# The first of two kinds of VectorE additions in a joint weight set no longer pinned to the order of the program

## The chip, the cores and the metric

The kernel runs on one core of a Trainium2 chip. The metric is the device time of one execution in microseconds (us); lower is better. The engines are TensorE (PE in the profile; its weight loads are PEld), VectorE (DVE), ScalarE (ACT), GpSimd (POOL) and SyncE (SP); the last two mostly issue DMAs here.

## The reference

One layer of a decoder trunk on 256 tokens with a width of 2048, in float32. Cut to what matters:

```python
h = rmsnorm(x, pre_norm_g)
proj = h @ w_in                       # (256, 2048) @ (2048, 18448)
a_q, a_k, a_v, a_g, a_lr, b_q, b_k, b_v, b_g, m_a, m_b = split(proj)
y_a = (rmsnorm(gla_chunked(a_q, a_k, a_v, gk)) * silu(a_g)) @ w_branch_a
y_b = (rmsnorm(diff_attention(b_q, b_k, b_v, lam)) * silu(b_g)) @ w_branch_b
merged = sigmoid(m_a) * y_a + sigmoid(m_b) * y_b
x = x + rmsnorm(merged @ w_out, post_norm_g)
```

The change is in the projection `h @ w_in`, which takes over half of the kernel's time.

## The kernel before, in words

Every matrix product is made of three products of rounded numbers: a weight tile is split into `hi` (a copy on ScalarE into the rounded type float32r, line 354) and `lo` (the tile minus `hi`, on VectorE, line 355), and TensorE multiplies the activations with both (line 551, a helper called for nearly all matmuls). Such a tile has 128 partitions and mostly 1024 columns. The tiles for `hi` and `lo` rotate through three buffers each, and the conversion runs three steps ahead of TensorE (`AHEAD`).

Nine stretches of the projection, the *sets* 0 to 8 (lines 220 to 261 and `block_products`), use a scheme that needs seven block products instead of eight: the 2048 x 1024 weights of a set are four blocks, and some products take sums of blocks. The seven products run in the order 1, 3, 5, 6, 2, 7, 4; each has four steps, written here as (product, t, h) with t and h of 0 or 1: t is a half of the block's rows and selects a tile, h a half of that tile's columns. Between a set's steps come steps of other column groups (`phase_steps`), whose raw tiles need no sums: in the profile they write banks named `bg`, the set's own `mm`.

The sums of weight blocks are made in place. For each t, a tile `a` is loaded with the first block and a tile `b` with the fourth (`link`), `c` with the third.

- After step (1, t, h) the second block is added to `a` by an accumulating DMA that POOL issues (line 249): (5, t, h) then reads `a`.
- After products 3 and 5 have read them, VectorE adds `b`, the fourth block, to `a` (line 257). Product 6 reads `a` then. This is called when the step in the table of `follow_set` has been written out: the additions for t = 0, halves h = 0 and 1, at (5, 1, 0) and (5, 1, 1); those for t = 1 at (6, 0, 0) and (6, 0, 1). Behind each, an accumulating DMA on POOL adds the second block to `b`, for product 7.
- At (7, t, h) VectorE adds `c`, the third block, to `a` (line 257 too), for product 4.

A scheduler orders each engine's instructions by its own model, so the order in which the program is written sets it only in part. `tc.keep_in_program_order(i)` pins an instruction behind the one that was written before it on its engine. TensorE's matmuls of this phase are all pinned so, as are POOL's DMAs, and in the kernel before all additions of line 257. The other names of the rows below are `q` and `k` (L793 to L796), results of the steps in between, `p` (L871, a copy of the bank of product 1 or 5 by ScalarE, and L874, a sum of such copies on VectorE), `gr` (L878 and L887, finished halves of a set), and L868 (ScalarE copies the bank of product 1 when that product is done, in sets 1 to 8). Line 291 is another addition of weight tiles, in the last part of the kernel.

Of the kernel before, what the change touches and what calls it, by code (L numbers as in the profile page):

```python
# [11 lines left out]
ALU = mybir.AluOpType  # L12
# [130 lines left out]
def hybrid_kernel(ctx: ExitStack, tc, xt, xn, preg, postg, w, w2, gkb, glag, lamv, diffg, ident_d, causal_d, lmask_d, out):  # L143
    nc = tc.nc
    pe, act, dve, pool, sp = nc.tensor, nc.scalar, nc.vector, nc.gpsimd, nc.sync
# [66 lines left out]
    raws = {}  # L212
    chain = {}
# [5 lines left out]
    def block(s, i, t):  # L219
        return weights(f"set{s}", 2 * i + t)[0]  # L220
# [24 lines left out]
    def follow_set(s, prod, t, h):  # L245
        c = slice(1024 * h, 1024 * h + 1024)

        def accumulate(name, i):
            tc.keep_in_program_order(pool.dma_start(chain[s, name, i][:, c], block(s, 1, i)[:, c], accum_op=ALU.add))  # L249

        if prod == 1:
            accumulate("a", t)
        i = {(5, 1): 0, (6, 0): 1, (7, 0): 0, (7, 1): 1}.get((prod, t))
        if i is not None:
            a = chain[s, "a", i][:, c]
            second = prod != 7
            tc.keep_in_program_order(dve.tensor_tensor(out=a, in0=a, in1=chain[s, "b", i][:, c] if second else raws[s, i, h], op=ALU.add))  # L257
            if second:
                accumulate("b", i)

    def part_link(s, name, make=u2):
        first, second = {"b": (3, None), "f": (3, 1), "e": (1, 0)}[name]
        for h in range(2):
            c = slice(1024 * h, 1024 * h + 1024)
            t = chain[s, name, h] = make([P, 1024], f"part_{name}")
            tc.keep_in_program_order(sp.dma_start(t, weights(s, first)[0][:, c]))
            if second is not None:
                tc.keep_in_program_order(pool.dma_start(t, weights(s, second)[0][:, c], accum_op=ALU.add))
# [53 lines left out]
    def emit_half():  # L322
# [33 lines left out]
        if joined:  # L356
            follow_set(*e[1:])
# [1215 lines left out]
    for c in range(2):  # L1573
# [12 lines left out]
        else:  # L1586
            end = ps("bg")
            c = slice(TURNED[0] % 1024, TURNED[0] % 1024 + 512)
# [68 lines left out]
```

## Time and profile before

| | |
|---|---|
| Time, median of 3 runs | 1090.64 us (1090.23 to 1091.9) |
| The profiled execution | 1089.85 us, its span 1088.0 us |
| TensorE busy | 1077.3 us (99%) |
| VectorE busy | 947.8 us (87%) |
| ScalarE busy | 742.4 us (68%) |
| POOL busy | 168.2 us (15%) |
| Granted TensorE clock | 0.999 of full speed |
| DMA | 293.44 MB, mean 270 GB/s |

A row of the timeline reads: start, duration, engine, line, operation, what it writes and reads, shapes, how many such instructions follow each other, and in brackets the idle time of the engine before it and what ended that. VectorE's and ScalarE's instructions overlap a little, so an instruction of 1.22 us can start 1.14 us behind the one in front. A row of the chain reads: start, duration, what. TensorE counts as busy while a matmul is in its pipeline, so its 99% don't mean that it lost only 1%; lost time is seen in the starts of its matmuls. The sets run from about 85 to 600 us.

### The profile page before, as it was taken

How to read it: one execution, taken by the hardware profiler on the slowest of the kernel's cores; microseconds unless marked ns; L12 is line 12 of the kernel's file. 1: busy time of each engine (PE TensorE's matmuls, PEld its weight loads, DVE VectorE, ACT ScalarE, POOL GpSimd, SP SyncE). 2: the span in 40 equal slices, each digit the busy share in tenths (PEclk: the TensorE clock that was granted, in tenths of full speed). 3: DMA queues.
4: the chain of work that ended last, by engine and by line, in shares of the span. 5: the costliest groups of instructions: out<-in, count | busy, mean ns of one | idle time of the engine just before them, and what ended most of it. 6: DMA issues, size and time to landing. Idle time of an engine off the chain costs nothing.

```text
span 1088.0 us, 15371 instructions
## 1 busy us (share of the span) xinstructions
PE 1077.3 (99%) x5404; PEld 918.0 (84%) x5404; DVE 947.8 (87%) x1282; ACT 742.4 (68%) x1068; POOL 168.2 (15%) x249
## 2 busy tenths in 40 slices
PE   9999999999999999999999999999999999999997
PEld 8998887878887888888888888888888888888886
DVE  7788989889998989898989899987778878879886
ACT  7987767777676767767776655566777776566662
POOL 0202121111212111212212210031011011100000
PEclk9999999999999999999999999999999999999999
DMA  8899799999897989898989776599897798988752
GB/s 347 271 340 285 226 288 283 256 269 300 230 344 173 358 184 374 197 335 218 316 240 273 273 258 202 194 321 315 277 299 257 272 297 269 325 300 260 273 190 99
DMA packets 67213, 293.44 MB, mean 270 GB/s; under 512 B 8704, under 2 KB 11776, under 8 KB 49984
## 3 DMA queue, kind: packets, MB, share of 16 engines
q1 hardware_dynamic: 38656, 174.29, 45.3%
q0 software_dynamic: 27904, 117.45, 40.2%
q8 instruction: 42, 0.69, 0.2%
q10 hardware_dynamic: 576, 0.73, 0.2%
q14 instruction: 35, 0.29, 0.1%
HBM read 265.17 MB, written 27.26 MB: 269 GB/s over the span
## 4 chain that ended last, share of the span: by engine, by line
PE 89%; DVE 5%; issue 2%; DMA 2%; ACT 1%; POOL 0%; POOLq 0%; SPq 0%; DVEq 0%; ACTq 0%
PE mm L551 60%; PE bg L551 18%; DVE lo L355 3%; PE mm L539 2%; PE bg L539 2%; DMA a<-in_w_dram 1%; DVE a L257 1%; PE mm L524 1%; PE bg L980 1%; PE bg L524 1%; PE bg L1147 0%; PE bg L1121 0%; DMA raw<-in_w_dram 0%; PE bg L1122 0%; PE bg L1159 0%
## 5 line engine op out<-in xcount | busy, mean ns | idle before, releaser
L354 ACT ACTIVATE hi<-raw 128x1024 fp32r<-128x1024 f32 (+3 forms) x229 | 234.6, 1028 | 148.9 <-PE mm L551 73.4
L355 DVE TENSOR_TENSOR lo<-raw,hi 128x1024 fp32r<-128x1024 f32 (+3 forms) x231 | 271.3, 1180 | 34.9 <-ACT hi L354 31.9
L354 ACT ACTIVATE hi<-a 128x1024 fp32r<-128x1024 f32 x144 | 152.5, 1060 | 63.1 <-PE mm L551 25.4
L355 DVE TENSOR_TENSOR lo<-a,hi 128x1024 fp32r<-128x1024 f32 x144 | 172.7, 1222 | 19.5 <-ACT hi L354 17.0
L551 PE MATMUL mm<-hi,xs 128*128 128x512 f32 (+1 forms) x688 | 174.8, 383 | 0.0
L551 PEld LDWEIGHTS mm<-hi,xs 128*128 128x128 f32 x688 | 128.5, 188 | 21.4
L551 PE MATMUL bg<-xs,hi 128*128 128x512 f32 x448 | 115.7, 390 | 0.0
L355 DVE TENSOR_TENSOR lo<-b,hi 128x1024 fp32r<-128x1024 f32 x72 | 88.0, 1223 | 18.0 <-ACT hi L354 15.9
L551 PE MATMUL mm<-lo,xs 128*128 128x512 f32 (+1 forms) x344 | 98.7, 383 | 0.1
L551 PEld LDWEIGHTS bg<-xs,hi 128*128 128x128 f32 x448 | 84.3, 188 | 16.6
L354 ACT ACTIVATE hi<-b 128x1024 fp32r<-128x1024 f32 x72 | 76.1, 1060 | 25.5 <-PE mm L551 13.5
L551 PE MATMUL mm<-xs,hi 128*128 128x512 f32 x320 | 84.9, 397 | 0.0
L551 PEld LDWEIGHTS mm<-lo,xs 128*128 128x128 f32 x344 | 64.2, 188 | 12.2 <-DVE lo L355 1.3
L551 PEld LDWEIGHTS bg<-xs,lo 128*128 128x128 f32 x448 | 60.3, 190 | 10.5 <-DVE lo L355 6.8
L551 PE MATMUL bg<-xs,lo 128*128 128x256 f32 x448 | 63.5, 285 | 2.6 <-DVE lo L355 2.4
L551 PEld LDWEIGHTS mm<-xs,hi 128*128 128x128 f32 x320 | 57.7, 189 | 9.6
L249 POOL DMA_DIRECT2D b<-in_w_dram x36 | 31.0, 861 | 169.1 <-ACT hi L354 70.1
L354 ACT ACTIVATE hi<-c 128x1024 fp32r<-128x1024 f32 x36 | 38.2, 1062 | 21.0 <-PE bg L551 9.7
L551 PE MATMUL mm<-hi,oah 128*128 128x512 f32 x128 | 50.9, 397 | 0.0
L551 PE MATMUL mm<-hi,oal 128*128 128x512 f32 x128 | 50.1, 391 | 0.0
L551 PEld LDWEIGHTS mm<-xs,lo 128*128 128x128 f32 x320 | 43.7, 190 | 3.2
L551 PE MATMUL mm<-xs,lo 128*128 128x256 f32 x320 | 44.6, 283 | 0.0
(410 smaller groups left out, 2218.6 us busy)
## 6 DMA issues: line engine op xcount, KB each, us to landing
raw<-in_w_dram SPq DMA_DIRECT2D x98, 1024.0 KB, 7.0
c<-in_w_dram SPq DMA_DIRECT2D x36, 512.0 KB, 8.4
a<-in_w_dram POOLq DMA_DIRECT2D x36, 512.0 KB, 9.8
b<-in_w_dram POOLq DMA_DIRECT2D x36, 512.0 KB, 8.4
a<-in_w_dram POOLq DMA_DIRECT2D x16, 1024.0 KB, 10.6
b<-in_w_dram POOLq DMA_DIRECT2D x16, 1024.0 KB, 7.9
raw<-in_w_dram SPq DMA_DIRECT2D x14, 832.0 KB, 7.1
gr<-gr POOLq DMA_DIRECT2D x9, 512.0 KB, 10.1
```

The lines of the kernel that those rows point to most:

```text
L249: tc.keep_in_program_order(pool.dma_start(chain[s, name, i][:, c], block(s, 1, i)[:, c], accum_op=ALU.add))
L257: tc.keep_in_program_order(dve.tensor_tensor(out=a, in0=a, in1=chain[s, "b", i][:, c] if second else raws[s, i, h], op=ALU.add))
L354: act.activation(hi_t[:, a:b], r[:, a:b], AF.Copy)
L355: dve.tensor_tensor(out=lo_t[:, a:b], in0=r[:, a:b], in1=f32(hi_t[:, a:b]), op=ALU.subtract)
L524: i = pe.matmul(out, lhs, rhs, start=first and n == 0, stop=last and n == len(pairs) - 1, **kw)
L539: i = pe.matmul(banks[g][b][:, :n], a[part][:, P * b : P * b + P], w[:, n * g : n * g + n], start=first, stop=last)
L551: i = pe.matmul(*args, **kw)
L980: pe.matmul(o, xk[:, P * c : P * c + P], xq.rearrange("p (b c t) -> p b c t", b=2, c=4)[:, :, c, :], start=i == 0, stop=i == 1)
```

## The change

Of the additions of line 257, only those of `c` (at product 7) are still pinned. Those of `b`, with which the sums for product 6 are made, are left to the scheduler.

```diff
@@ follow_set
             second = prod != 7
-            tc.keep_in_program_order(dve.tensor_tensor(out=a, in0=a, in1=chain[s, "b", i][:, c] if second else raws[s, i, h], op=ALU.add))
+            add = dve.tensor_tensor(out=a, in0=a, in1=chain[s, "b", i][:, c] if second else raws[s, i, h], op=ALU.add)
             if second:
                 accumulate("b", i)
+            else:
+                tc.keep_in_program_order(add)
```

The order of TensorE, POOL and SP stays. Lines behind 257 have their numbers raised by 2 in the changed kernel (355 becomes 357). VectorE in set 2 before, from the lo's of (5, 0, 0) and (5, 0, 1) on; `a_1712` is the tile of t = 0, `a_1826` that of t = 1, `raw` a tile of the steps in between:

```order
L355 TENSOR_TENSOR lo_2056<-a_1712,hi_2055 128x1024
L355 TENSOR_TENSOR lo_2066<-a_1712,hi_2065 128x1024
L355 TENSOR_TENSOR lo_2078<-a_1826,hi_2077 128x1024
L257 TENSOR_TENSOR a_1712<-a_1712,b_1871 128x1024
L794 TENSOR_TENSOR q_2012<-bg_2013,q_2012 128x2x128
L355 TENSOR_TENSOR lo_2107<-a_1826,hi_2106 128x1024
L257 TENSOR_TENSOR a_1712<-a_1712,b_1871 128x1024
L355 TENSOR_TENSOR lo_2119<-raw_2102,hi_2118 128x1024
L355 TENSOR_TENSOR lo_2131<-a_1712,hi_2130 128x1024
```

And in the changed kernel:

```order
L357 TENSOR_TENSOR lo_2056<-a_1712,hi_2055 128x1024
L257 TENSOR_TENSOR a_1712<-a_1712,b_1871 128x1024
L357 TENSOR_TENSOR lo_2066<-a_1712,hi_2065 128x1024
L257 TENSOR_TENSOR a_1712<-a_1712,b_1871 128x1024
L357 TENSOR_TENSOR lo_2078<-a_1826,hi_2077 128x1024
L796 TENSOR_TENSOR q_2012<-bg_2013,q_2012 128x2x128
L357 TENSOR_TENSOR lo_2107<-a_1826,hi_2106 128x1024
L357 TENSOR_TENSOR lo_2119<-raw_2102,hi_2118 128x1024
L357 TENSOR_TENSOR lo_2131<-a_1712,hi_2130 128x1024
```

Each addition now stands right behind the lo that reads its half of the tile last. Sets 4 and 6 are ordered in the same way. In sets 1, 3, 5 and 7 the two additions go up by one row each, in set 0 the first by two rows and the second by one, and in set 8 only the first, by two. In sets 3 and 5 the first addition of t = 1 also goes up by one row.

VectorE in product 7 of set 7, where `gr` is the addition of line 887 and `raw` the tile of a step in between, before:

```order
L257 TENSOR_TENSOR a_4312<-a_4312,c_4634 128x1024
L887 TENSOR_TENSOR gr_4742<-mm_4451,p_301_4648 128x512
L355 TENSOR_TENSOR lo_4848<-raw_4776,hi_4847 128x1024
L355 TENSOR_TENSOR lo_4870<-a_4189,hi_4869 128x1024
L355 TENSOR_TENSOR lo_4880<-a_4189,hi_4879 128x1024
```

And in the changed kernel:

```order
L257 TENSOR_TENSOR a_4312<-a_4312,c_4634 128x1024
L357 TENSOR_TENSOR lo_4848<-raw_4776,hi_4847 128x1024
L889 TENSOR_TENSOR gr_4742<-mm_4451,p_301_4648 128x512
L357 TENSOR_TENSOR lo_4870<-a_4189,hi_4869 128x1024
L357 TENSOR_TENSOR lo_4880<-a_4189,hi_4879 128x1024
```

The lo of the raw tile passes the addition that finishes a half of the set.

ScalarE in set 2, from the hi of a raw tile to that of the next, before:

```order
L354 ACTIVATE hi_2118<-raw_2102 128x1024
L354 ACTIVATE hi_2130<-a_1712 128x1024
L871 ACTIVATE p_157_2156<-mm_2101 128x512
L354 ACTIVATE hi_2144<-a_1712 128x1024
L354 ACTIVATE hi_2161<-raw_2102 128x1024
```

And in the changed kernel, as also in sets 4 and 6:

```order
L356 ACTIVATE hi_2118<-raw_2102 128x1024
L356 ACTIVATE hi_2130<-a_1712 128x1024
L356 ACTIVATE hi_2144<-a_1712 128x1024
L873 ACTIVATE p_157_2156<-mm_2101 128x512
L356 ACTIVATE hi_2161<-raw_2102 128x1024
```

The copy of product 5's bank goes behind the hi of (6, 0, 1).

## The prediction

> **What bounds the kernel now.** I read the page first, then the times of one ScalarE row that comes once in every set, then the timeline of VectorE, ScalarE and TensorE at one place. The page, with the chain that ended last:
>
> ```profile
> span 1088.0 us, 15371 instructions
> ...
> PE 89%; DVE 5%; issue 2%; DMA 2%; ACT 1%; POOL 0%; POOLq 0%; SPq 0%; DVEq 0%; ACTq 0%
> ```
>
> TensorE carries 89% of the chain, so a shorter VectorE or DMA is worth nothing except where TensorE stands and waits for it. What can be won is therefore the time that TensorE loses in the sets, and this is found by a clock inside the kernel. Line L868 (a bank copied when product 1 of a set is done) runs once in each of the sets 1 to 8, right behind TensorE. The columns are start, duration, and the instruction:
>
> ```profile
> 148.95 0.58 ACT L868 ACTIVATE mm<-mm 128x512 f32<-128x512 f32 x1
> 207.91 0.58 ACT L868 ACTIVATE mm<-mm 128x512 f32<-128x512 f32 x1
> 266.80 0.58 ACT L868 ACTIVATE mm<-mm 128x512 f32<-128x512 f32 x1
> 324.43 0.58 ACT L868 ACTIVATE mm<-mm 128x512 f32<-128x512 f32 x1
> 383.65 0.58 ACT L868 ACTIVATE mm<-mm 128x512 f32<-128x512 f32 x1
> 441.29 0.58 ACT L868 ACTIVATE mm<-mm 128x512 f32<-128x512 f32 x1
> 500.89 0.58 ACT L868 ACTIVATE mm<-mm 128x512 f32<-128x512 f32 x1
> 559.12 0.58 ACT L868 ACTIVATE mm<-mm 128x512 f32<-128x512 f32 x1
> ```
>
> The differences are 58.96, 58.89, 57.63, 59.22, 57.64, 59.60 and 58.23 us for the sets 1 to 7. The matmuls of these sets are equal in number and shape. Sets 3 and 5 agree at 57.63, which I take as the period without a stall. The others lose 1.33, 1.26, 1.59, 1.97 and 0.60, together 6.75 us, and no later set gives any of it back.
>
> Where set 2 loses it is seen on VectorE around products 5 and 6. Call (5,0,1) the step with product 5, t = 0, h = 1:
>
> ```profile
> 214.91 2.58 DVE L355 TENSOR_TENSOR lo<-a,hi 128x1024 fp32r<-128x1024 f32 x2
> 219.49 1.23 DVE L355 TENSOR_TENSOR lo<-a,hi 128x1024 fp32r<-128x1024 f32 x1 [2.00 <-ACT hi L354]
> 220.63 1.22 DVE L257 TENSOR_TENSOR a<-a,b 128x1024 f32<-128x1024 f32 x1
> ...
> 222.10 1.22 DVE L355 TENSOR_TENSOR lo<-a,hi 128x1024 fp32r<-128x1024 f32 x1
> 223.24 1.22 DVE L257 TENSOR_TENSOR a<-a,b 128x1024 f32<-128x1024 f32 x1
> 224.37 1.22 DVE L355 TENSOR_TENSOR lo<-raw,hi 128x1024 fp32r<-128x1024 f32 x1
> ...
> 228.91 1.22 DVE L257 TENSOR_TENSOR a<-a,b 128x1024 f32<-128x1024 f32 x1
> 230.04 0.69 DVE L874 TENSOR_TENSOR p<-mm,p 128x512 f32<-128x512 f32 x1
> 230.65 1.22 DVE L355 TENSOR_TENSOR lo<-raw,hi 128x1024 fp32r<-128x1024 f32 x1
> ```
>
> The first row is the lo of (5,0,0) and (5,0,1); then VectorE stands idle for 2.00 us until ScalarE brings the hi of (5,1,0). From there to 231.9 it runs without a gap, with one instruction of 128x1024 every 1.14 us. Four additions (L257) are in this stretch. TensorE over the same time, and from the chain the time of a block of 16 that waits for nothing:
>
> ```profile
> 220.49 0.62 PE L551 MATMUL mm<-lo,r1h 128*128 128x512 f32 x2
> ...
> 229.62 1.78 PE L551 MATMUL bg<-xs,hi 128*128 128x512 f32 x7
> 231.92 1.22 PE L551 MATMUL bg<-xs,lo 128*128 128x256 f32 x8 [0.52 <-DVE lo L355]
> ...
> 233.21 0.40 PE L551 MATMUL mm<-hi,s2h 128*128 128x512 f32 x1
> ...
> 188.17 2.77 PE bg L551 x16
> ```
>
> TensorE takes the lo of (5,0,1) at 220.49, 3.0 us after VectorE had it (214.91 + 2.58 = 217.49). The block of 16 from 229.62 to 233.21 took 3.59 instead of 2.77 us, since its lo came at 231.87, the end of the last VectorE row above. So VectorE is 3 us ahead, idles, and 14 us later is late by 0.8 us.
>
> **The change part by part.** No instruction is added or removed except two that only wait; TensorE's, POOL's and SP's orders stay. VectorE's moves, and three pairs on ScalarE.
>
> *Sets 2, 4 and 6.* The two additions of half h = 0 and h = 1 go in front of the lo of (5,1,0). Requeued for set 2 with the spacings of the rows: lo (5,0,0) ends at 216.14; addition 216.17 to 217.39; lo (5,0,1) 217.31 to 218.53, still 2.0 us ahead of TensorE's 220.49; second addition 218.56 to 219.78, so the hole of 2.00 is filled; lo (5,1,0) at 219.70 instead of 219.49; after it the first addition is missing from the row, so lo (5,1,1) comes at 221.17 instead of 222.10, and the raw lo, without the second, at 222.31 instead of 224.37. From there on everything is 2.06 us earlier as long as ScalarE is. ScalarE:
>
> ```profile
> 222.09 1.06 ACT L354 ACTIVATE hi<-a 128x1024 fp32r<-128x1024 f32 x1 [0.35 <-PE mm L551]
> 224.15 0.60 ACT L871 ACTIVATE p<-mm 128x512 f32<-128x512 f32 x1 [0.99 <-PE mm L551]
> ...
> 225.97 1.06 ACT L354 ACTIVATE hi<-raw 128x1024 fp32r<-128x1024 f32 x1 [0.28 <-PE bg L551]
> ```
>
> The hi of the last raw lo is there at 227.03, so that lo can start at 228.6 and end at 229.8. TensorE asks for it after eight matmuls of hi, about 231.0 by the rows above and some 0.4 earlier when its own small stalls before (1.26 - 0.82) are gone. It is ahead by 0.8 us, and the stall goes. The swap on ScalarE (p behind the hi of (6,0,1)) delays p by about 1.0 us, to 225.8; its reader on VectorE (L874, 230.04, then about 228) is later still, so it costs nothing. Worth: 1.26 for set 2 and 1.59 for set 4. Set 6 has the same order as set 4; I take 1.59 of its 1.97 and leave the rest, which I don't ascribe to this place.
>
> *Sets 1, 3, 5 and 7.* Each of the two additions goes up by one row. Sets 3 and 5 lose nothing now and gain nothing. Set 1 waits for data too:
>
> ```profile
> 163.44 0.50 PE L551 MATMUL mm<-hi,r1h 128*128 128x512 f32 x1
> ...
> 165.26 1.09 PE L551 MATMUL bg<-xs,hi 128*128 128x512 f32 x4
> ...
> 146.68 15.54 DMA a<-in_w_dram
> 162.33 1.07 ACT hi L354
> ```
>
> The hi of (5,1,1) waits for a landing at 162.22; six matmuls take 1.82 us, where half a 12-matmul piece of 2.75 is 1.37. These 0.45 us stay, and 0.88 of set 1's 1.33 go, since the addition that stands between that lo and the next is already done. In set 7 the same reordering also brings one raw lo in front of the addition of L887 in product 7, the place of its 0.60 us; I take all of it.
>
> *Sets 0 and 8*, which the clock doesn't cover, lose at the same place:
>
> ```profile
> 113.93 1.00 PE L551 MATMUL bg<-lo,xs 128*128 128x400 f32 x4 [0.15 <-DVE lo L355]
> ...
> 577.61 1.98 PE L551 MATMUL bg<-xs,hi 128*128 128x512 f32 x8
> ...
> 580.78 0.40 PE L551 MATMUL mm<-hi,s2h 128*128 128x512 f32 x1
> ```
>
> Set 8's block takes 3.17 instead of 2.77: 0.40. Of set 0 the row shows at least 0.15; by the ratio of loss to idle in set 2 (0.82 to 0.52) I take 0.25.
>
> *The new waits.* Eight additions (one in sets 0 and 8, two in 2, 4 and 6) now stand right behind the lo that reads the same half of the tile, and have to wait for its end. The nearest rows are a pair of that kind late in the kernel:
>
> ```profile
> 922.38 1.22 DVE L355 TENSOR_TENSOR lo<-part_e,hi 128x1024 fp32r<-128x1024 f32 x1
> 923.63 1.23 DVE L291 TENSOR_TENSOR part_e<-part_e,raw 128x1024 f32<-128x1024 f32 x1
> 924.77 2.35 DVE L355 TENSOR_TENSOR lo<-raw,hi 128x1024 fp32r<-128x1024 f32 x2
> ```
>
> The waiting one starts 1.25 us behind its forerunner, the free one 1.14: 0.11 each, 0.9 us of VectorE in all. It lies in the hole, which covers it; without that cover it would be 0.9 us of TensorE. The Trainium skill ("VectorE: DVE Perf Modes", section "The DRAIN you can't avoid") says that a semaphore between chained VectorE operations costs nothing extra. By it this term would be 0 instead of 0.9 us; the rows here disagree.
>
> *POOL.* Behind each addition an accumulating DMA of block 1 into the same b tile is queued on POOL, in unchanged order. It starts 2 to 4 us earlier; product 7 reads b long after, so that is no gain. Its cost, if any, is in a rival below.
>
> Sum: 0.25 + 0.88 + 1.26 + 1.59 + 1.59 + 0.60 + 0.40 = 6.6 us. Against the profiled execution's 1089.85 that is 1083.3. The median of the runs lies 0.8 above it, so I predict 1084.0.
>
> **Rivals.** *A landing takes the gain.* The accumulating DMA of b now falls into the last part of those of a, for which (5,1,0) and (5,1,1) wait. For: set 1's landing took 15.54 us and already holds TensorE. Against: in the whole program ScalarE waits for such a landing once:
>
> ```profile
> ACT hi L354 <- DMA a<-in_w_dram: 2.8, 1, 2.8
> ...
> HBM read 265.17 MB, written 27.26 MB: 269 GB/s over the span
> ```
>
> Both kinds are issued by POOL, the later behind the earlier. Price: 512 KB at the mean of 269 GB/s are 1.9 us; in two sets (1, and a second one with as little room) that is 3.8 us, leaving 2.8: 1087.8. The Trainium skill ("DMA: Bandwidth & Descriptors", section "Issuing engines are not separate DMA queues") says that transfers of all issuing engines interleave on the same 16 engines, which would make this likelier; no row here shows b slowing a.
>
> *The stall only moves.* If VectorE's whole load, not its order, made it late, the loss would reappear a few steps on: 1090.6. Against: sets 3 and 5 carry the same lo's and additions and lose nothing.
>
> *Slower.* In sets 0, 2, 4, 6 and 8 an addition now holds the lo of (5,0,1) back by up to 1.25 us. If TensorE takes it sooner than in set 2, it waits there: five places by 1.25, less the 1.48 of sets 1 and 7, gives +4.8: 1095.4. It decides where the room is under 1.05 us; set 2 has 3.0. Set 8, where data come late, would show it first.
>
> **How the numbers follow.** The main case has 0.76, with a range of its own from 1082.6 (all 6.75 and the 0.65 of sets 0 and 8 from the fastest run, 1090.23, is 1082.8, and 0.2 for the scatter of a median) to 1085.8. The landing has 0.11, the stall that moves 0.07, the slower case 0.06. The range of 1082.6 to 1088.6 holds the first two. A difference of 0.2%, 2.2 us, is about what a measurement of this kernel can tell from none; below 1088.4 lie the main case and most of the landing's, 0.85 in all; within 0.2% 0.09; slower 0.06.
>
> **What would show it.** In the trace of the changed kernel the L868 rows of sets 2, 4 and 6 should lie 57.6 to 58.0 us apart and those of sets 3 and 5 still 57.6; the hole of 2.00 us behind the lo's of (5,0,h) should hold additions; TensorE's idle time before bg, ended by lo of L355, should fall from 0.52 in such a set to none. The prediction is wrong if ScalarE's waits for landings of a grow, if periods of sets 3 or 5 rise, or if TensorE waits for the lo of (5,0,1).

## The result and the profile after

The changed kernel takes 1084.38 us (median of 4 runs, 1083.6 to 1085.57); the kernel before took 1090.74 (4 runs beside them, 1090.23 to 1091.9). The ratio is 0.9941, with a 95% interval from 0.9924 to 0.9958: 6.4 us faster, as forecast in size (1084.0). The profiled execution took 1084.9 us. Its page, first line and chain:

```profile
span 1083.1 us, 15373 instructions
...
PE 82%; issue 8%; DVE 4%; DMA 4%; POOL 1%; ACT 1%; POOLq 0%; SPq 0%; DVEq 0%; ACTq 0%
```

TensorE's share of the chain has fallen, though it stalls less. This is because the chain is followed back from one late wait, for a transfer, which is shown below; from there it runs along POOL's queue between 640 and 720 us, and the stretches between that queue's instructions, of up to 11.71 us, count as "issue". The clock of the sets tells more. It is the row that was L868, now L870 (start, duration, instruction):

```profile
148.24 0.58 ACT L870 ACTIVATE mm<-mm 128x512 f32<-128x512 f32 x1
206.63 0.58 ACT L870 ACTIVATE mm<-mm 128x512 f32<-128x512 f32 x1
264.26 0.58 ACT L870 ACTIVATE mm<-mm 128x512 f32<-128x512 f32 x1
321.90 0.58 ACT L870 ACTIVATE mm<-mm 128x512 f32<-128x512 f32 x1
379.53 0.58 ACT L870 ACTIVATE mm<-mm 128x512 f32<-128x512 f32 x1
437.16 0.58 ACT L870 ACTIVATE mm<-mm 128x512 f32<-128x512 f32 x1
495.16 0.58 ACT L870 ACTIVATE mm<-mm 128x512 f32<-128x512 f32 x1
552.79 0.58 ACT L870 ACTIVATE mm<-mm 128x512 f32<-128x512 f32 x1
```

The periods of the sets 1 to 7 are now 58.39, 57.63, 57.64, 57.63, 57.63, 58.00 and 57.63 us. Sets 2, 4 and 7 have come down to the period of sets 3 and 5; set 6 keeps 0.37 and set 1 keeps 0.76. The last row is 6.33 us earlier than in the kernel before. Of this, 0.29 us had been there already at 112 us, ahead of the first stall that the change removes, and is scatter (the even-sets kernel and the pinned kernel without transfers below are 0.65 and 0.69 us earlier there).

VectorE in set 2, from the lo of (5,0,0) on:

```profile
213.63 1.23 DVE L357 TENSOR_TENSOR lo<-a,hi 128x1024 fp32r<-128x1024 f32 x1
214.89 1.23 DVE L257 TENSOR_TENSOR a<-a,b 128x1024 f32<-128x1024 f32 x1
216.03 1.22 DVE L357 TENSOR_TENSOR lo<-a,hi 128x1024 fp32r<-128x1024 f32 x1
217.28 1.22 DVE L257 TENSOR_TENSOR a<-a,b 128x1024 f32<-128x1024 f32 x1
218.43 1.22 DVE L357 TENSOR_TENSOR lo<-a,hi 128x1024 fp32r<-128x1024 f32 x1
...
221.03 1.22 DVE L357 TENSOR_TENSOR lo<-raw,hi 128x1024 fp32r<-128x1024 f32 x1
222.16 1.22 DVE L357 TENSOR_TENSOR lo<-a,hi 128x1024 fp32r<-128x1024 f32 x1
```

There is no idle time in brackets any more: the two additions fill the hole of 2.00 us. The lo of (5,1,0) starts 4.80 us behind that of (5,0,0), before 4.58. The raw lo, two rows on, starts 7.40 us behind it, before 9.46. TensorE over the same time:

```profile
219.21 0.62 PE L553 MATMUL mm<-lo,r1h 128*128 128x512 f32 x2
...
227.90 1.75 PE L553 MATMUL bg<-xs,hi 128*128 128x512 f32 x7
229.48 1.12 PE L553 MATMUL bg<-xs,lo 128*128 128x256 f32 x8
230.44 0.40 PE L553 MATMUL bg<-xs,hi 128*128 128x512 f32 x1
```

It takes the lo of (5,0,1) at 219.21, and that lo was done at 217.25, so there were 2.0 us left. The block of 16 that had waited 0.52 us runs through, from 227.90 to 230.67, in 2.77 us. Over all sets, TensorE's waits before `bg`, in the view of waits from 85 to 640 us (us in total, times, longest), first of the kernel before and then of the changed one:

```profile
PE bg L551 <- DVE lo L355: 2.6, 7, 0.5
```

```profile
PE bg L553 <- DVE lo L357: 0.3, 1, 0.3
```

These idle times are smaller than the time lost, since TensorE still counts as busy while the matmuls ahead are in its pipeline.

Two things took some of the gain back. One is the landing of `a` in set 1, for whose halves ScalarE now waits 1.34 and 2.81 us, before once for 2.8 (ScalarE's timeline, then two pieces of the chain):

```profile
157.91 1.06 ACT L356 ACTIVATE hi<-a 128x1024 fp32r<-128x1024 f32 x1 [1.34 <-DMA a<-in_w_dram]
161.78 1.06 ACT L356 ACTIVATE hi<-a 128x1024 fp32r<-128x1024 f32 x1 [2.81 <-DMA a<-in_w_dram]
```

```profile
145.97 15.70 DMA a<-in_w_dram
...
719.73 12.95 DMA vback<-vl
```

The other is the second piece, behind the sets. TensorE waits for a spilled tile that is read back:

```profile
732.72 0.50 PE L526 MATMUL bg<-vback,ath 128*128 128x512 f32 x1 [1.45 <-DMA vback<-vl]
```

### The profile page after: what moved, and what is told of

Same layout as the page of the kernel before. It is cut to its first block, busy times and chain, and to the rows that moved or that the text cites. A ratio compares the mean times of both kernels' runs of the same rounds, so it can differ in the third digit from the quotient of the medians.

```text
span 1083.1 us, 15373 instructions
## 1 busy us (share of the span) xinstructions
PE 1073.0 (99%) x5404; PEld 918.2 (85%) x5404; DVE 947.9 (88%) x1282; ACT 741.9 (68%) x1068; POOL 168.1 (16%) x249
## 4 chain that ended last, share of the span: by engine, by line
PE 82%; issue 8%; DVE 4%; DMA 4%; POOL 1%; ACT 1%; POOLq 0%; SPq 0%; DVEq 0%; ACTq 0%
PE mm L553 55%; PE bg L553 20%; DVE lo L357 2%; PE mm L541 2%; PE bg L541 2%; DMA a<-in_w_dram 1%; DMA vback<-vl 1%; DMA raw<-in_w_dram 1%; PE bg L1149 0%; PE bg L1123 0%; PE bg L526 0%; PE bg L1124 0%; POOL dl L177 0%; DVE keep L357 0%; PE bg L1162 0%
## 5 line engine op out<-in xcount | busy, mean ns | idle before, releaser
L357 DVE TENSOR_TENSOR lo<-c,hi 128x1024 fp32r<-128x1024 f32 x36 | 43.0, 1218 | 4.6 <-ACT hi L356 4.6
```

The lines of the kernel that those rows point to most:

```text
L357: dve.tensor_tensor(out=lo_t[:, a:b], in0=r[:, a:b], in1=f32(hi_t[:, a:b]), op=ALU.subtract)
```

## The experiments

In all of them the ratio is to the kernel before, run beside them on the same chip: 1090.70 us for the first four below (down to the first run with both additions in the hole), 1090.34 for that kernel's second run, the changed kernel again, the changed kernel without the transfers into `b` and the one with all additions free, and 1090.27 for the other four.

**The even sets alone.** Freed in sets 2, 4 and 6 only (diff against the changed kernel).

```diff
-            else:
+            if not second or s not in (2, 4, 6):
                 tc.keep_in_program_order(add)
```

> The changed order in sets 2, 4 and 6 alone; the additions of the other sets stay pinned as before. Theory (in each set the lateness of VectorE goes when the additions stand in its idle hole, and each set's gain is its own): periods of L868 in sets 2, 4, 6 fall to 57.6, 57.6, 58.0 us and those of sets 1 and 7 stay at 58.9 and 58.2; together 4.5 us, so about 1086.2. Rival (the gain comes from elsewhere, such as the additions of all sets or the swap in set 7): under 2 us. Rival (the wait for vback of 1.4 us in the trace of the changed kernel belongs to the change): it shows here too.

1086.13 us (1085.51 to 1087.49), ratio 0.9959 (0.9946 to 0.9971). The periods of sets 2, 4 and 6 are 57.63, 57.63 and 58.00, as in the changed kernel, so the three terms of 4.4 us stand; set 7 keeps its loss (58.23). Two periods were not foreseen. Set 5, still pinned, takes 58.36 here and took 57.64 in the kernel before; its trace has a wait of 0.27 us for a lo at 404.49, where the kernel before has none. And set 1 takes 59.63, not 58.9: ScalarE waited 1.96 and 2.70 us for the halves of `a`.

**Order without additions.** The kernel before with the additions of `b` for t = 0 left out (product 6 then lacks this term).

```diff
-            tc.keep_in_program_order(dve.tensor_tensor(out=a, ...))
+            if prod != 5:
+                tc.keep_in_program_order(dve.tensor_tensor(out=a, ...))
```

> The order of before with the additions of the fourth block to the tile of t = 0 left out (18 instructions of 1.22 us, 22 us of VectorE; the result is another). Theory (the reordering hides these additions wholly): the same time as the changed kernel within 1 us, 1083.5 to 1085. Rival (VectorE's load, not its order, makes the stalls, and reordering takes only a part): 2 us or more below the changed kernel.

1084.46 us (1083.9 to 1085.43), ratio 0.9943 (0.993 to 0.9956): the changed kernel's time. VectorE in set 2:

```profile
213.58 2.59 DVE L356 TENSOR_TENSOR lo<-a,hi 128x1024 fp32r<-128x1024 f32 x2
218.16 1.23 DVE L356 TENSOR_TENSOR lo<-a,hi 128x1024 fp32r<-128x1024 f32 x1 [2.00 <-ACT hi L355]
...
220.77 1.22 DVE L356 TENSOR_TENSOR lo<-raw,hi 128x1024 fp32r<-128x1024 f32 x1
```

The hole is empty again, and the raw lo starts 7.19 us behind the lo of (5,0,0), against 7.40 in the changed kernel. So in their new place these additions and their self-waits cost the kernel nothing that the runs can tell; in their old place they had cost 6.2 us, the whole gain.

**The additions later.** The kernel before, with the additions written behind the raw step that follows product 5, so that none of t = 0 stands between two lo's of product 5.

```diff
-            tc.keep_in_program_order(dve.tensor_tensor(out=a, ...))
-            if second:
-                accumulate("b", i)
+            def add():
+                tc.keep_in_program_order(dve.tensor_tensor(out=a, ...))
+                if second:
+                    accumulate("b", i)
+            later.append(add) if prod == 5 else add()
...
         if joined:
             follow_set(*e[1:])
+        else:
+            while later:
+                later.pop(0)()
```

> All pinned; the two additions of t = 0 go the other way, behind the raw lo that stands between products 5 and 6. The lo's of (5,1,1) and of that raw tile are then as early as in the changed kernel, but the hole stays empty. Theory (the hole is what gives the time back): the small stalls of 0.3 to 0.4 us ahead of the raw block go, the stall of 0.8 us at the next raw block stays, and hi of (6,0,0) now waits for an addition: 1 us faster to 3 us slower than before. Rival (it is enough that the additions don't stand between the lo's of product 5): as fast as the changed kernel, 6 us less than before.

1097.97 us (1097.59 to 1099.59), ratio 1.007 (1.0058 to 1.0082): 7.3 us slower, where little was expected. VectorE, TensorE, and TensorE's largest group of waits (85 to 640 us):

```profile
225.54 2.35 DVE L258 TENSOR_TENSOR a<-a,b 128x1024 f32<-128x1024 f32 x2
...
228.42 1.22 DVE L359 TENSOR_TENSOR lo<-a,hi 128x1024 fp32r<-128x1024 f32 x1
```

```profile
231.96 0.73 PE L558 MATMUL mm<-lo,s2h 128*128 128x512 f32 x2 [0.61 <-DVE lo L359]
```

```profile
PE mm L558 <- DVE lo L359: 6.0, 13, 0.6
```

Both additions now stand in front of the lo's of product 6, which TensorE takes as soon as they are done, and sets 3 and 5 lose too (58.44 and 58.42). So the cost isn't tied to the place between the lo's of product 5: this other place behind VectorE's hole costs more. The 7.3 us are not VectorE's alone. The hi's of product 6 now wait for these additions as well (ScalarE's waits for such additions in the sets are 18.3 us, before 10.7), and its waits for landings of `a` grew from 2.8 to 7.9 us. What each is worth was not separated.

**Both in the hole, pinned.** The kernel before, with both additions for t = 0 written at step (5,0,1).

```diff
-        i = {(5, 1): 0, (6, 0): 1, (7, 0): 0, (7, 1): 1}.get((prod, t))
+        i = {(5, 0): 0, (6, 0): 1, (7, 0): 0, (7, 1): 1}.get((prod, t))
...
-        if i is not None:
+        if i is not None and (prod != 5 or h):
...
+            for g in (0, 1) if prod == 5 else (h,):
```

> All additions pinned, but both of t = 0 are written at step (5,0,1) instead of (5,1,0) and (5,1,1): they stand together behind the lo of (5,0,1), in the hole, in every set. No addition stands right behind the lo that it must wait for. Theory (what counts is that they stand in front of the lo of (5,1,0)): the same as the changed kernel, 6.0 to 6.9 us less than before, except set 7's 0.6 us if its stall came from the swap of gr and the raw lo. Rival (freedom of the scheduler on other instructions makes the gain): under 3 us. Rival (the immediate waits cost something on the path): 0.3 to 0.9 us faster than the changed kernel.

1087.03 us (nine runs from 1083.45 to 1090.09), ratio 0.9964 (0.9951 to 0.9976). In its profile, of the execution of 1083.45, all of the sets 1 to 7 but set 1 (57.83) and set 6 (58.00) are at 57.63 or 57.64, though every addition is pinned. The median is 2.6 us above the changed kernel's, so the theory's "the same" missed. Why the other executions took up to 6.6 us more was asked by running it again.

> The kernel with all additions pinned and both additions for t = 0 written at product 5, second half first step, once more. Its nine runs lay between 1083.45 and 1090.09, far wider than any other here, and its profile was of the fastest. TensorE's and SyncE's orders are those of the changed kernel; what differs is that the second accumulation into b is issued about 1.3 us earlier. If the scatter is that transfer's meeting with a's landing in set 1, a profile of a run near the median (1087) shows the loss as one ACT wait for the DMA of a of 3 to 5 us in set 1, and the other periods at 57.6. If it is spread, several sets are above 58. If it is a late wait for vl, it stands at 719 us. Median again 1086 to 1088, range at least 4 us.

1086.48 us (1085.6 to 1087.87). The profiled execution took 1085.6, and none of the three guesses holds: set 1 takes 58.33 and the wait for `vl` is absent. The new loss lies at 611 us, in ScalarE's queue. Of this run (POOL, ScalarE, TensorE):

```profile
603.44 0.55 POOL L177 DMA_DIRECT2D dl<-dk  x1 [1.06 <-DVE dk L774]
```

```profile
611.31 1.28 ACT L955 ACT_TABLE_LOAD   x1 [6.88 <-DMA dl<-dk]
```

```profile
614.26 2.12 PE L553 MATMUL mm<-hi,xs 128*128 128x512 f32 x8 [1.87 <-ACT hi L356]
```

And of the changed kernel:

```profile
602.60 0.55 POOL L177 DMA_DIRECT2D dl<-dk  x1
```

```profile
605.62 1.28 ACT L955 ACT_TABLE_LOAD   x1 [0.96 <-DMA dl<-dk]
```

Behind the sets this kernel's scheduled order differs a little from the changed one's: the spill of `dk` is issued 0.8 us later, and landed after 7.9 us instead of 3.0. ScalarE stands for it with the hi's queued behind. In the execution of 1083.45 it landed after 5.6 us and TensorE did not wait. These two profiles are 0.03 us apart at the clock's last row (551.93 and 551.96) and 2.2 us at their ends; that the slower runs up to 1090 have the same cause was not seen.

**The changed kernel again.**

> The changed kernel itself, once more. Its first profile had one new wait of 1.45 us at 719 us, for the landing of vl in vback, in a place where the kernel before and two of the variants have none (their landings took up to 12.5 us, this one 12.95). If that wait belongs to the change, it stands in this profile too, with over 1 us, and the span is again about 4.9 under that of before. If it is the scatter of a landing, the profile has less than 0.5 there and the span is 1081.5 to 1082.5. Time either way 1084.4 within 0.7.

1083.88 us (1083.44 to 1084.93), ratio 0.9937 (0.9925 to 0.9949). TensorE does not wait for `vl` this time, so that wait is the scatter of a landing (it stands in two other kernels here, with 0.5 us in the one with later additions and 1.90 in the one with set 0 free). But the span is again 1083.2, not the 1081.5 to 1082.5 expected of that case, since set 1 took 59.26: TensorE stood still for the hi of the late half of `a`.

```profile
163.61 0.50 PE L553 MATMUL mm<-hi,r1h 128*128 128x512 f32 x1 [0.99 <-ACT hi L356]
```

**Without the transfers into b.** The changed kernel, and the kernel before, each with the accumulating transfers into `b` for t = 0 left out (product 7 then lacks this term).

In the changed kernel, whose additions of `b` stay free:

```diff
-            if second:
+            if second and prod == 5:
+                pass
+            elif second:
                 accumulate("b", i)
```

In the kernel before:

```diff
-            if second:
+            if second and prod != 5:
                 accumulate("b", i)
```

> The changed kernel with the accumulating transfers into b for t = 0 left out (two of 512 KB for each set; the output misses that link). Theory: the change's gain is VectorE's order, and these transfers, which the change lets start earlier, do only harm: they run beside the landing of a's second half in set 1, where ACT's hi still waits 0.7 us for it. Without them set 1 loses under 0.2 there, all periods but set 7's are 57.63, and the time is 1083.3 to 1084.0. Rival: these transfers take nothing from a's landing (other queues' traffic does), and the time is that of the changed kernel, 1084.4 within 0.4. Second rival: the gain of the change came from starting them earlier, so that leaving them out gives several us more: 1082 or less.

> The kernel before with the accumulating transfers into b for t = 0 left out and all additions in program order (the output misses that link). In the changed kernel leaving them out was worth 0.5 to 1.0 us. Theory: VectorE's order is the cause of before's waits and these transfers are not, so the periods of sets 2, 4 and 6 stay at 58.9 to 59.6 and the time is 1089.5 to 1090.7. Rival: the transfers' meeting with others makes up a good part of what the change brought; then the periods fall to under 58.3 and the time to 1087 or less.

The changed kernel so edited: 1083.36 us (1082.35 to 1085.63), ratio 0.9935 (0.9922 to 0.9947). The kernel before: 1089.88 (1088.86 to 1091.07), ratio 0.9996 (0.9987 to 1.0004), with sets 2, 4 and 6 at 58.89, 59.22 and 59.59. So the gain doesn't come from these transfers. Whether they slow the landing of `a` is not shown: set 1 still takes 58.22 without them, where under 57.83 was expected, and the 0.5 to 1.0 us by which the changed kernel so edited is faster are within the spread of the runs.

**Without the transfers into a in set 1.** This prices the landing itself (set 1 then lacks the term).

```diff
-        if prod == 1:
+        if prod == 1 and s != 1:
             accumulate("a", t)
```

> The changed kernel with the accumulating transfers into a left out in set 1 alone (four of 512 KB; the output misses that link). This prices the landing that set 1 waits for. Theory: nothing lands last there any more, set 1's period falls from 58.4 to 59.3 to 57.63, and the time by 0.8 to 1.6 us: 1082.5 to 1083.4. Rival: the other transfers of that stretch take its place as the last to land, or VectorE does, and the period stays over 58.2 and the time within 0.4 of 1084.1.

1082.44 us (1081.29 to 1082.6), ratio 0.9924 (0.991 to 0.9938). Set 1 takes 57.64: its remaining loss, 0.76 and 1.63 us in the two profiles of the changed kernel, goes with these transfers. The stretch from 145 to 162 us (length, busy time and count of PE, PEld, DVE, ACT, POOL, granted clock, DMA share, GB/s), in the changed kernel and here:

```profile
145.00:162.00 17.00, 17.00 (x84) 14.35 (x83) 14.16 (x14) 9.98 (x12) 2.10 (x4) 1.00 1.03 268
```

```profile
145.00:162.00 17.00, 17.00 (x84) 14.38 (x83) 14.74 (x15) 11.61 (x13) 1.21 (x2) 1.00 0.57 191
```

With these transfers the share of the 16 DMA engines in this stretch is 1.03, without them 0.57.

**The third block's additions free too.** The changed kernel with them freed in all sets, then in set 0 alone, then in set 0 together with the edit just shown.

```diff
-            else:
-                tc.keep_in_program_order(add)
```

> The additions of the third block are freed as well, so no addition of this line is held to program order any more. After the change TensorE still waits for a lo in two places that the traces put down to pinned additions of c at product 7: in set 0 between 126 and 137 us (1.65 us in all, the rows mm<-lo,r3h and bg<-xs,lo behind them) and in set 6 at 468.7 (0.34). Theory: the same mechanism acts there, so freeing them takes up to 2.0 us more: 1082.4 to 1083.2, against 1084.4 of the changed kernel. Rival 1: the scheduler now puts additions of c ahead of lo's that are needed sooner, as in the run with the late additions, but at product 7: TensorE gains 0.3 to 0.8 us of waits in each set and the time is 1086 to 1090. Rival 2: nothing, 1084.4, because what stands last at 126 to 137 us is a landing and not VectorE.

1085.9 us (1084.35 to 1088.52), ratio 0.9957 (0.9943 to 0.9971): 1.5 to 2.0 above the changed kernel, by the medians (the intervals overlap a little), and so neither the gain expected nor quite the first rival's. Its clock's first rows, and the first of the new waits:

```profile
146.74 0.58 ACT L868 ACTIVATE mm<-mm 128x512 f32<-128x512 f32 x1
206.57 0.58 ACT L868 ACTIVATE mm<-mm 128x512 f32<-128x512 f32 x1
265.02 0.58 ACT L868 ACTIVATE mm<-mm 128x512 f32<-128x512 f32 x1
```

```profile
236.26 0.74 PE L551 MATMUL mm<-lo,xs 128*128 128x512 f32 x2 [0.42 <-DVE lo L355]
```

Set 0 is done 1.50 us earlier, and set 1 ends about where it ended with the changed kernel (206.57 against 206.63). The landing took 0.86 us of it (TensorE's first matmul behind it starts 0.64 us earlier, the ones ahead of it had been 1.50), and a wait for a lo at 178 us another 0.47. Set 2 takes 58.45, with a new wait in the product where additions of `c` had been moved up.

```diff
-            else:
+            elif s:
                 tc.keep_in_program_order(add)
```

> The changed kernel with the additions of the third block freed in set 0 alone. With all of them free, set 0's first row came at 146.74 us in place of 148.24, but set 1 grew as much (59.83), since its second half of a landed at 161.03 and 161.67 us whether it was issued at 144.47 or at 145.97; and sets 2 and 6 and the stages behind lost 0.5 to 0.9 us each to VectorE's new order. Here sets 1 to 7 keep the changed kernel's order. Theory: set 0 gives 1.5 us, of which the landing in set 1 leaves 0.2 to 1.0, so 1083.0 to 1083.9. Rival: nothing of it stays (1084.1 within 0.3), or all of it (1082.6).

> Both edits in one: set 0's additions of the third block free, and the transfers into a left out in set 1 (the output misses that link). If the landing in set 1 is what takes set 0's 1.5 us, they pass through here: first row at 146.7, set 1 at 57.63, and the time 1.3 to 1.7 under that of the kernel with the transfers left out alone, 1081.0 to 1082.0. If something else behind takes them, the two are within 0.5 of each other.

Set 0 alone: 1083.09 us (1080.78 to 1085.21), ratio 0.9932 (0.9917 to 0.9947), as expected and the lowest median of the kernels that leave nothing out. Its interval overlaps that of the changed kernel, so it isn't shown to be better. With the landing taken away: 1080.57 (1080.15 to 1080.83), ratio 0.991 (0.9897 to 0.9924), 1.9 us under the kernel with the landing taken away alone, a little more than the 1.3 to 1.7 expected; its first row is at 146.38 against 147.96, and set 1 takes 57.63 and 57.64. So the 1.6 us won in set 0 pass through once nothing lands late behind it.

## Why the prediction was right, point by point

The mechanism is the one predicted, and it is shown. Additions placed into VectorE's hole cost nothing (the kernel without them takes the same time), behind the hole they cost (the kernel with later additions), and TensorE's waits before `bg` fell from 2.6 to 0.3 us. In sets 2, 4 and 6 it is the place and not the freedom of the scheduler: with both additions pinned in the hole their periods are those of the changed kernel (57.63, 57.63 and 58.00). No run separates the swap on ScalarE, which comes along in sets 2, 4 and 6 wherever the stall is gone. But before, the hi of the late lo in set 2 was there at 227.03, 3.6 us before VectorE began that lo (230.65), so VectorE did not wait for ScalarE there.

*Sets 2, 4, 6 and 7.* 1.26, 1.59, 1.60 and 0.60 us by the two clocks, predicted 1.26, 1.59, 1.59 and 0.60. The requeued rows of set 2 came out too: the raw lo is 2.06 us earlier against the lo of (5,0,0), as predicted, and the lo of (5,0,1) has 2.0 us left. The 0.37 left in set 6 are those not ascribed to this place. Set 7's 0.60 is another place: before, TensorE stands in product 7 for the raw lo that comes behind the addition of L887.

```profile
546.21 1.22 PE L551 MATMUL bg<-xs,lo 128*128 128x256 f32 x8 [0.33 <-DVE lo L355]
```

The wait is gone where the raw lo stands in front, in the changed kernel and, with all additions pinned, in the one with both in the hole (set 7 at 57.63). In the even-sets kernel the old order and the wait are still there. So this 0.60 comes from a swap that the scheduler makes along with the change, as the prediction had it.

*Sets 0 and 8.* Set 0's block of 12 (8 with hi and 4 with lo) in TensorE's timeline, first before, then after:

```profile
112.17 1.61 PE L551 MATMUL bg<-hi,xs 128*128 128x400 f32 x8
...
114.77 0.40 PE L551 MATMUL mm<-hi,s2h 128*128 128x512 f32 x1
```

```profile
111.88 1.61 PE L553 MATMUL bg<-hi,xs 128*128 128x400 f32 x8
...
114.06 0.40 PE L553 MATMUL mm<-hi,s2h 128*128 128x512 f32 x1
```

2.60 us became 2.18: 0.42, where 0.25 had been taken by the ratio of loss to idle. The same block before, set against one that waits for nothing (107.22 to 109.40, 2.18 us), would have given the right number. Set 8's block now takes 2.78 us (571.26 to 574.04), 0.39 less.

*Set 1* is the mis-sized term: 0.88 predicted, 0.57 measured here, and none in the second profile (59.26 against 58.96 before). The traces split it at TensorE's first matmul on the late half of `a`, at 163.44 us before and 162.89 after. From there to the first matmul of (6,1,0) (174.31 and 173.03) it took 10.87 us before and 10.14 after; in the second profile it is 10.11 (163.61 to 173.72), and in the even-sets kernel, where set 1 is still pinned, 10.87 (163.41 to 174.28). So the additions' new place won 0.73 to 0.76 us here, and not none. What differs is the stretch ahead, from the set's first row to that matmul: 14.49 us before, 14.65 after and 15.54 in the second profile. I had left 0.45 to the landing as if it were a fixed loss. But the data landed 13.27, 13.43 and 14.33 us behind the first row in these three, and the later they land, the more of the gain turns into waiting here.

*The sum.* The places give 6.43 us by the profiles, predicted 6.6. The pair of profiled executions differs by 4.95 only, mainly because of the wait of 1.45 us for `vl`, which no step had; in the profile taken again it is absent. By medians the gain is 6.4. That the sum is so close is in part luck: set 0 was taken 0.17 too low and set 1 0.31 too high.

*The self-waits.* The lo at 213.63 and the addition behind it at 214.89 are 1.26 us apart, the next two (214.89 and 216.03) 1.14. So they do cost about 0.11 us each on VectorE. The Trainium skill ("VectorE: DVE Perf Modes", section "The DRAIN you can't avoid") says that such a semaphore costs nothing extra; this trace disagrees on VectorE's time. The kernel's time can't show it, since the hole covers it.

*The rivals.* The landing took 0.8 to 1.6 us in set 1, not the 3.8 of that rival, and the transfers into `b` that it blamed are not shown to be its cause. The stall did not move on. TensorE never waited for the lo of (5,0,1) in set 2, and no period rose but set 1's in the second profile. One sign that had been named against the prediction did show: ScalarE's waits for landings of `a` grew. They cost part of set 1's term and no more.

## What to carry to other kernels

Look for the place where an engine that sets the pace later on stands idle for lack of input, and put into it the work that only has to be done some time before its reader: here two additions of 1.22 us, put some 14 us ahead of the stall, were worth 1.3 to 1.6 us in each of three sets. A pin that holds such work in written order can cost as much as leaving the work out would win, as here, but taking away all pins was worse by the medians than taking away one kind. And size a wait for a landing by the time at which the data arrive, not by its length: what is won ahead of it can be lost there, and how much changes from one execution to the next.

## What the runs showed of the hardware

- A transfer issued earlier need not land as much earlier. The last accumulating DMA into `a` of set 1 was issued at 146.68 (before), 145.97 (after), 145.79 (the changed kernel again), 144.47 (all free) and 143.26 us (set 0 free) and took 15.54, 15.70, 16.61, 16.57 and 16.21 us. It landed at 162.22, 161.67, 162.40, 161.04 and 159.47. From 145 to 162 us the DMA share was 1.03 or 1.04 before, after, in the changed kernel again and with set 0 free. Two profiles of the same kernel differ by 0.73 us in the landing, so a single pair says little.
- In the profile of the kernel with set 0 free, TensorE waited 1.90 us for `vl` and was then granted a lower clock. Two windows of it (columns as above), the first from just before the end of the wait at 731.32:

```profile
731.00:734.00 3.00, 2.69 (x8) 2.17 (x9) 1.29 (x3) 0.69 (x2) 0.00 (x0) 0.69 1.23 276
734.00:737.00 3.00, 3.00 (x12) 2.40 (x12) 0.91 (x3) 1.34 (x4) 1.24 (x2) 0.74 0.73 161
```

  In windows of 0.5 us it is 0.66 from 732.0, 0.50 from 732.5 to 735.5 and 0.93 in the next one: half the clock for about 3.4 us, begun 0.8 us behind the wait. Waits of 1.87 us (at 614 us, both additions pinned in the hole) and of 1.45 us (the changed kernel) were followed by 1.00. The Trainium skill ("TensorE: Matmul & The Clock Gate", section "Part 1: The HAM clock gate (the "warmup" mystery)") puts the idle time after which the clock drops at about 3.4 us; here it dropped once after 1.90. What set it off is open.
